# A decoder layer on one core: another engine for the first rounding, one dummy product fewer, and an even cut of the last tile

## The chip, the cores and the metric

The kernel runs on one core of a Trainium2 chip. The metric is the device time in microseconds of one execution. Three runs of the kernel before the change gave 946.8, 948.13 and 947.93 us; the median is 947.93 us.

## The reference

One layer of a decoder trunk on 512 tokens with 1024 features, in float32:

```python
h = rmsnorm(x, ln1)
q, k, v, r, a, att, gates = split(h @ w_in)
y_gla = gated_linear_attention(q, k, v, a, r) @ w_o_gla
y_att = dilated_attention(att) @ w_o_attn           # three groups of heads
x = x + (sigmoid(g_gla) * y_gla + sigmoid(g_att) * y_att) @ w_out
x = x + square(relu(rmsnorm(x, ln2) @ w_mlp1)) @ w_mlp2
x = x + sigmoid(rmsnorm(x, ln3) @ w_pg) * (p @ w_pp)
out = rmsnorm(x, ln_f)
```

Two places matter here: the very first product, 512 columns of `w_in` (the queries of the first attention group) with `x`, and the very last, `w_pg` with the normalized `x`, followed by the sigmoid gate, the addition, the last norm and the store.

## The kernel before

**Products in three terms.** TensorE multiplies operands that are rounded to fp32r. To keep float32's accuracy every operand is split into `hi`, its rounded value, and `lo`, the rounded remainder, and every product is three: hi·hi, hi·lo and lo·hi. As a rule ScalarE writes `hi` (a copy that rounds) and VectorE writes `lo` (a subtraction). Many of the middle matrix products go by a seven-product scheme on quarters of the matrices; the first and the last product do not.

**The order of the work.** The program is written out by hand in its order for each engine; every engine runs its own list in that order and waits where an operand is missing. Weights come through SyncE's DMA queue (some sums of weights through GpSimd's) a few tiles ahead of their use.

**The start (L541 to L596).** SyncE issues eight pairs of tiles, `xr[k]` (128 features by 512 tokens of transposed `x`) and `wr[k]` (128 features by 512 columns of weights), 256 KB each, and ScalarE's queue loads the small vectors `cv`. Meanwhile TensorE does `NWARM` dummy products of a 128x128 tile of ones with itself (L566). Each dummy leaves two records in the trace. Then, for each k:

- ScalarE: `xh`, the rounded `x` times the norm's weight (through `split_hi`, L476); `hi`, the rounded `wr[k]` (L579); later the square of `x` for the norm (L504).
- VectorE: the remainder of `x` (through `split_into`, L304), then `lo`, the remainder of `wr[k]` (L581); later the running sum of squares (L585).
- TensorE (L594): 12 products of 512 columns, four output tiles by three terms. For k = 0 they are sorted by term: the first four need `hi` and `xh`, the next four the remainder of `x`, the last four `lo`.

**The end (L1708 to L1772).** The last product runs tile of tokens by tile of tokens, in the order `TTS` = 2, 3, 0, 1, first for the left 512 output columns (`pg0`), then for the right ones (`pg1`). For each tile, 8 slices of features by three terms are 24 products of 512 columns. A finished tile goes through `gated_all`: `gate` on ScalarE (sigmoid, L1710), a multiplication and an addition on VectorE (L1716, L1717), the sum of squares on ScalarE (L1721). For the right half `scale_out` then finishes the norm: VectorE adds up (L1735), GpSimd takes the power (L1736), ScalarE scales the left half (L1738) and its DMA is issued, and `put` scales the right half on VectorE and stores it (L1744, L1746).

The last tile of all (L1758 to L1772) is cut at column `LAST`. Each part has its own 24 products in its own PSUM tile. The gate of the first part is issued after the first part's products, its multiplication and addition follow on VectorE, then comes the second part's gate; the squares of the first part stand on ScalarE behind that gate:

```python
    parts, sgs = [slice(0, LAST), slice(LAST, 512)], []
    for c in parts:
        ...
        sgs.append(gate(ps, n, tt))
        if c.start == 0:
            gated(sgs[0], 4 + tt, c)
    squares(sgs[0], 4 + tt, parts[0], 8)
    gated(sgs[1], 4 + tt, parts[1])
    V.tensor_scalar(sp2[:, tt:tt + 1], ss2[:, 8:9], sp2[:, tt:tt + 1], None, op0=OP.add)
    squares(sgs[1], 4 + tt, parts[1], 9)
    scale_out(tt, 9)
```

Of the kernel before, what the change touches and what calls it, by code (L numbers as in the profile page):

```python
# [13 lines left out]
AF = mybir.ActivationFunctionType  # L14
# [165 lines left out]

NRAW = 8

LAST = 384

TTS = (2, 3, 0, 1)

NWARM = 9


@with_exitstack  # L190
def block_kernel(ctx, tc, xT, x, ws, pT, wts, wha, wa2, vec, lnf, rel, onehot, ident_d, mask_d, out):
    nc = tc.nc
    V, S, TE, SY, GP = nc.vector, nc.scalar, nc.tensor, nc.sync, nc.gpsimd
# [15 lines left out]
    def u32r(name="ur"):  # L209
        return ar.tile([P, T], F32R, tag="u", name=name)  # L210
# [4 lines left out]
    def smt():  # L215
        return sm.tile([P, T], F32, tag="sm", name="smt")
# [254 lines left out]
    def split_hi(x, col=None):  # L471
        hi = u32r()
        if col is None:
            S.activation(hi, x, AF.Copy)  # L474
        else:
            S.activation(hi, x, AF.Copy, scale=col)  # L476
        return hi

    def split_lo(x, hi, col=None):
        lo = u32r()  # L480
        split_into(lo, x, hi, col)
        return hi, lo
# [18 lines left out]
    def square(x):  # L501

        t = u32()
        S.activation(t, x, AF.Square, scale=1.0 / 32.0)  # L504
        return t
# [42 lines left out]
    xr, wr = [], []  # L548
# [15 lines left out]
    pw = smt()  # L564
    for _ in range(NWARM):
        TE.matmul(pw[:, 0:P], lhsT=ones, rhs=ones, start=True, stop=True)  # L566
# [8 lines left out]
    for k in range(KC):  # L575
        x, ln = xr[k], cv[:, C_LN1 + k:C_LN1 + k + 1]
        hi, lo = u32r(), u32r()
        xh = split_hi(x, ln)
        S.activation(hi, wr[k], AF.Copy)  # L579
        xsr.append(split_lo(x, xh, ln))  # L580
        V.tensor_tensor(lo, wr[k], hi.bitcast(F32), op=OP.subtract)  # L581
        if k == 1:
            acc = sq
        elif k > 1:
            V.tensor_tensor(acc, acc, sq, op=OP.add)  # L585
        sq = square(x)
        xh, xl = xsr[k]

        terms = [(i, j) for i in range(NS) for j in range(3)]
        if not k:  # L590
            terms.sort(key=lambda t: t[1])
        for i, j in terms:
            c = slice(i * P, (i + 1) * P)
            TE.matmul(q0ps[i], lhsT=(hi, hi, lo)[j][:, c], rhs=(xh, xl, xh)[j], start=not k and not j,  # L594
                      stop=k == KC - 1 and j == 2)
# [1161 lines left out]

    parts, sgs = [slice(0, LAST), slice(LAST, 512)], []  # L1758
    for c in parts:
# [101 lines left out]
```

## Time and profile before

| | |
|---|---|
| median of three runs | 947.93 us (946.8 to 948.13) |
| the profiled execution | 946.6 us |
| its span in the profile | 944.8 us |
| TensorE, products | 936.2 us busy, 5860 records |
| VectorE | 737.9 us busy |
| ScalarE | 555.6 us busy |
| GpSimd | 113.2 us busy |
| DMA | 158.75 MB, 168 GB/s on average |

The profile is of one execution; its times are counted from the start of the span. PE is TensorE's products, PEld its loads of the stationary operand, DVE VectorE, ACT ScalarE, POOL GpSimd, SPq, ACTq and POOLq the queues in which SyncE, ScalarE and GpSimd issue DMAs. A row of the timeline gives the start, the duration, the engine, the line, the operation, the tiles written and read, their shapes, how many instructions are merged in it, and in brackets the engine's idle time before it and what ended that. A row of the grouped view gives the count, the total busy time, the mean duration in ns, and idle time. Products are pipelined, so their durations overlap; their pace is read from the distances of their starts.

### The profile page before, as it was taken

To read this page: it belongs to the slowest core of one execution; us is meant where nothing else is said; L and a number is where in the kernel's file an instruction comes from. 1 tells how busy PE (TensorE), PEld (TensorE's weight loads), DVE (VectorE), ACT (ScalarE), POOL (GpSimd) and SP (SyncE) were. 2 spreads that over 40 slices of the span, in tenths; PEclk is the share of its full clock that TensorE was granted. 3 is DMA by queue.
4 is the path that set the end of the run, shared out by engine and by line. 5 is a ranking of instruction groups with operands and counts; after the bars stand their busy time and mean duration, and the time that the engine had idled before them with its cause. 6 is when DMAs were issued, how large, how long until landed. Compare 5 with 4: busy or idle time off the path is not lost.

```text
span 944.8 us, 15151 instructions
## 1 busy us (share of the span) xinstructions
PE 936.2 (99%) x5860; PEld 844.8 (89%) x5860; DVE 737.9 (78%) x1040; ACT 555.6 (59%) x918; POOL 113.2 (12%) x157
## 2 busy tenths in 40 slices
PE   9999999999999999999999999999999999999996
PEld 8789998899988888999988889999999888888886
DVE  7698869866789579978968779776677789897664
ACT  7357546545675578775743578665556536655543
POOL 0150010120100012022100300100000101021000
PEclk9999999999999999999999999999999999999999
DMA  9474482873817456555654788666546718599202
GB/s 356 141 234 113 133 202 68 280 237 109 189 58 212 166 134 201 135 134 179 183 148 116 177 216 256 161 172 179 157 112 166 191 49 194 148 268 368 88 1 90
DMA packets 49354, 158.75 MB, mean 168 GB/s; under 512 B 7108, under 2 KB 7696, under 8 KB 49281
## 3 DMA queue, kind: packets, MB, share of 16 engines
q1 hardware_dynamic: 31104, 103.76, 31.6%
q0 software_dynamic: 14496, 49.51, 26.5%
q10 hardware_dynamic: 3680, 4.51, 1.3%
q8 instruction: 46, 0.75, 0.3%
q14 instruction: 28, 0.22, 0.1%
HBM read 149.32 MB, written 10.26 MB: 169 GB/s over the span
## 4 chain that ended last, share of the span: by engine, by line
PE 96%; issue 1%; DVE 1%; DMA 1%; ACT 0%; POOL 0%; POOLq 0%; DVEq 0%; ACTq 0%
PE mmt L338 75%; PE smt L338 12%; PE mmt L594 2%; PE smt L1028 2%; DMA u<-y_dram 1%; PE smt L968 1%; PE smt L891 1%; PE smt L566 0%; PE smt L861 0%; PE smt L985 0%; PE smt L984 0%; PE smt L860 0%; PE smt L974 0%; PE smt L1412 0%; PE smt L1084 0%
## 5 line engine op out<-in xcount | busy, mean ns | idle before, releaser
L338 PE MATMUL mmt<-ur,hi 128*128 128x256 f32 (+1 forms) x2192 | 436.4, 297 | 0.0
L338 PEld LDWEIGHTS mmt<-ur,hi 128*128 128x128 f32 x2192 | 349.7, 189 | 11.8
L302 DVE TENSOR_TENSOR lo<-w,hi 128x1024 fp32r<-128x1024 f32 x254 | 308.6, 1219 | 60.5 <-PE mmt L338 37.0
L338 PE MATMUL mmt<-ur,lo 128*128 128x256 f32 (+1 forms) x1096 | 326.6, 298 | 0.5 <-DVE lo L302 0.5
L324 ACT ACTIVATE hi<-w 128x1024 fp32r<-128x1024 f32 x254 | 265.4, 1055 | 101.9 <-PE mmt L338 24.8
L338 PE MATMUL mmt<-hi,ur 128*128 128x512 f32 (+3 forms) x912 | 266.2, 375 | 0.0
L338 PEld LDWEIGHTS mmt<-ur,lo 128*128 128x128 f32 x1096 | 206.6, 189 | 6.3 <-DVE lo L302 0.7
L338 PEld LDWEIGHTS mmt<-hi,ur 128*128 128x128 f32 x912 | 165.3, 188 | 28.6
L338 PE MATMUL mmt<-lo,ur 128*128 128x512 f32 (+3 forms) x456 | 170.6, 374 | 0.0
L474 ACT ACTIVATE ur<-u 128x512 fp32r<-128x512 f32 x113 | 67.5, 625 | 65.3 <-DVE u L622 17.1
L338 PEld LDWEIGHTS mmt<-lo,ur 128*128 128x128 f32 x456 | 85.7, 188 | 15.1
L338 PE MATMUL smt<-hi,ur 128*128 128x512 f32 x288 | 89.1, 390 | 0.0
L302 DVE TENSOR_TENSOR ur<-u,ur 128x512 fp32r<-128x512 f32 x112 | 73.6, 685 | 10.8 <-ACT ur L474 10.2
L467 DVE TENSOR_TENSOR u<-u,mmt 128x512 f32<-128x512 f32 (+1 forms) x94 | 58.0, 648 | 27.2 <-PE mmt L338 26.9
L253 POOL DMA_DIRECT2D w<-in_wts_dram x46 | 43.5, 993 | 249.8 <-DMA w<-in_wts_dram 145.3
L408 ACT ACTIVATE u<-mmt 128x512 f32<-128x512 f32 x72 | 42.9, 596 | 51.0 <-PE mmt L338 50.8
L338 PEld LDWEIGHTS smt<-hi,ur 128*128 128x128 f32 x288 | 53.8, 188 | 10.9
L338 PE MATMUL smt<-lo,ur 128*128 128x512 f32 x144 | 56.0, 389 | 0.0
L281 POOL DMA_DIRECT2D w<-in_wts_dram x18 | 16.1, 894 | 282.0 <-DVE w L278 158.1
L338 PEld LDWEIGHTS smt<-lo,ur 128*128 128x128 f32 x144 | 27.0, 188 | 5.7
L1509 ACT ACTIVATE u<-u 128x512 f32<-128x512 f32 x24 | 15.0, 628 | 26.7 <-DVE u L1505 26.7
L844 ACT ACTIVATE u<-u,st 128x256 f32<-128x256 f32 (+1 forms) x32 | 15.6, 488 | 12.5 <-DVE st L840 11.0
(242 smaller groups left out, 848.0 us busy)
## 6 DMA issues: line engine op xcount, KB each, us to landing
w<-in_wts_dram SPq DMA_DIRECT2D x182, 512.0 KB, 5.1
w<-in_wts_dram POOLq DMA_DIRECT2D x70, 512.0 KB, 7.1
u<-in_xT_dram SPq DMA_DIRECT2D x8, 256.0 KB, 5.2
u<-in_ws_dram SPq DMA_DIRECT2D x8, 256.0 KB, 5.3
v_dram<-u ACTq DMA_DIRECT2D x8, 256.0 KB, 6.4
u<-v_dram POOLq DMA_DIRECT2D x8, 256.0 KB, 6.5
y_dram<-u ACTq DMA_DIRECT2D x8, 256.0 KB, 2.2
u<-y_dram POOLq DMA_DIRECT2D x8, 256.0 KB, 7.0
```

The lines of the kernel that those rows point to most:

```text
L253: GP.dma_start(w, wts[UNIT[b]], accum_op=OP.add)
L281: GP.dma_start(w, wts[UNIT[f"{q}.A21"]], accum_op=OP.add)
L302: V.tensor_tensor(lo, x, hi.bitcast(F32), op=OP.subtract)
L324: S.activation(hi[:, s], w[:, s], AF.Copy, scale=1.0 if c is None else c)
L338: TE.matmul(o, lhsT=l, rhs=r, start=a, stop=b, skip_group_check=shared)
L408: S.activation(sums[c], bank[b], AF.Copy, scale=-scale if c[0] else scale)
L467: V.tensor_tensor(out, s, ps, op=OP.subtract if m else OP.add)
L474: S.activation(hi, x, AF.Copy)
L594: TE.matmul(q0ps[i], lhsT=(hi, hi, lo)[j][:, c], rhs=(xh, xl, xh)[j], start=not k and not j, stop=k == KC - 1 and j == 2)
L844: S.activation(q3[:, a, s:], q3[:, a, s:], AF.Exp, bias=nm[:, col + a:col + a + 1], accum_out=sums[:, col + a:col + a + 1])
L1028: TE.matmul(o, lhsT=l[a][:, lc], rhs=r[b], start=start and i == 0, stop=stop and i == 2)
L1509: S.activation(s, s, AF.Square)
```

## The change

Three edits. In the first round of the start (k = 0) VectorE writes `hi` of the weights with `tensor_copy`, in its list ahead of the remainder of `x`; rounds 1 to 7 stay with ScalarE. There are 8 dummy products instead of 9. And the last tile of tokens is cut at column 256 instead of 384, so that both parts have 256 columns.

```diff
-LAST = 384
+LAST = 256
...
-NWARM = 9
+NWARM = 8
...
         xh = split_hi(x, ln)
-        S.activation(hi, wr[k], AF.Copy)
+        if k:
+            S.activation(hi, wr[k], AF.Copy)
+        else:
+            V.tensor_copy(hi, wr[k])
         xsr.append(split_lo(x, xh, ln))
         V.tensor_tensor(lo, wr[k], hi.bitcast(F32), op=OP.subtract)
```

## The prediction, made before the changed kernel was run

> **What bounds the kernel now.** I read the page first, then the chain of work that ended last, then the timeline of the two ends that the change touches: the first 9 us and the last 15.
>
> ```profile
> span 944.8 us, 15151 instructions
> PE 936.2 (99%) x5860; PEld 844.8 (89%) x5860; DVE 737.9 (78%) x1040; ACT 555.6 (59%) x918; POOL 113.2 (12%) x157
> PEclk9999999999999999999999999999999999999999
> PE 96%; issue 1%; DVE 1%; DMA 1%; ACT 0%; POOL 0%; POOLq 0%; DVEq 0%; ACTq 0%
> ```
>
> TensorE is busy 99% of the span and is 96% of the chain. So between its first product and its last one, work on other engines is worth nothing, and a shift of the first product is carried to the end. What can move the time is what lies before the first real product and after the last one, and how long the products take. The profiled execution took 946.6 us around its span of 944.8; the median of the three runs is 947.93 (946.8 to 948.13), 1.33 us more than the profiled one. I make the sum on the profiled execution and take its difference off the median.
>
> **The start.** Order of time on the chain, then the engines' rows around the first product (the page's timeline, start and duration in us):
>
> ```profile
> 1.00 4.21 PE smt L566 x18
> 5.21 22.16 PE mmt L594 x96
> ...
> 1.19 0.42 SPq L554 DMA_DIRECT2D u<-in_ws_dram  x1
> 3.76 0.72 ACT L476 ACTIVATE ur<-u,cv 128x512 fp32r<-128x512 f32 x1 [0.89 <-DMA cv<-in_vec_dram]
> 4.39 0.61 ACT L579 ACTIVATE ur<-u 128x512 fp32r<-128x512 f32 x1
> 4.52 0.75 DVE L304 SCALAR_TENSOR_TENSOR ur<-u,cv,ur 128x512 fp32r<-128x512 f32 x1 [3.65 <-ACT ur L476]
> 5.19 0.68 DVE L581 TENSOR_TENSOR ur<-u,ur 128x512 fp32r<-128x512 f32 x1
> ...
> 4.57 0.63 PE L566 MATMUL smt<-ones 128*128 128x128 f32 x2
> 4.79 0.42 PE L566 MATMUL smt<-ones 128*128 128x128 f32 x1
> 5.06 0.74 PE L594 MATMUL mmt<-ur 128*128 128x512 f32 x1
> 5.63 0.63 PE L594 MATMUL mmt<-ur 128*128 128x512 f32 x2
> 5.86 0.63 PE L594 MATMUL mmt<-ur 128*128 128x512 f32 x2
> ...
> u<-in_ws_dram SPq DMA_DIRECT2D x1, 256.0 KB, 3.1
> L1058 DVE COPY u<-u 128x256 f32<-128x256 f32 x4 | 1.2, 288 | 0.0
> L1505 DVE TENSOR_SCALAR u<-u 128x512 f32<-128x512 f32 x32 | 13.5, 424 | 0.5
> ```
>
> Nine dummies are 18 records, one every 0.21 us (4.57 to 4.79). The last takes its slot to about 5.00. The rounded weights `hi` come from ScalarE at 4.39 + 0.61 = 5.00. So two things release the first product at 5.06 at once, and taking away either alone gains nothing: the diff moves both.
>
> *One dummy fewer*: two records, 2 x 0.21 = 0.43 us; the array is free at 4.57.
>
> *Rounding on VectorE*: the tile lands at 1.19 + 3.1 = 4.29, and VectorE idles until 4.52, so the copy starts near 4.33. Its cost with an fp32r result has no row. Nearest are a plain copy of half the size (0.288) and a one-operand instruction of the same size in f32 (0.424); the upper bound is L581, two operands and an fp32r result, 0.68. I take 0.42, since the copy also reads one operand: `hi` at 4.75, first product at about 4.80, 0.25 us earlier. With 0.68 it would be ready at 5.01: nothing gained, 0.01 lost. The other operand is ready at 3.76 + 0.72 = 4.48, the floor, and would allow 0.5 us. The Trainium skill, "VectorE: DVE Perf Modes", section "Mode 2×_2P", says that a copy with a single source in SBUF gets two results a cycle even in fp32, while two-tensor instructions stay at one; the row for 256 columns (0.288, against 0.42 for two operands below) agrees for f32, and no run here shows it for an fp32r result.
>
> Behind the copy on VectorE stand L304 and L581 of the first tile. L304 goes from 4.52 to about 4.77, L581 ends near 6.12 instead of 5.87. Their readers are the fifth and the ninth product, which at 0.23 us a product after 5.86 come at 6.3 and 7.2: hidden. ScalarE loses 0.61 us of work, and its later tiles come no later. No DMA is moved past another; SP's and POOL's queues are untouched.
>
> *How much of 0.25 us survives.* The first product took from 5.06 to 5.63, the next from 5.63 to 5.86: the array was still slow until somewhere in that gap, though the page's clock line shows 9 throughout. The weight loads say the same:
>
> ```profile
> L566 PEld LDWEIGHTS smt<-ones x18: 288/333/338, 1.0 to 4.6; 128*128 128x128 f32 x18
> L594 PEld LDWEIGHTS mmt<-ur x96: 187/188/338, 5.1 to 26.8; 128*128 128x128 f32 x96
> ```
>
> If the clock rises at the same moment as now, products started earlier run slowly. At twice 0.227 us the second would start at 5.25 and the third at 5.71 instead of 5.86: 0.15 us gained. With the 0.57 us of the present first gap it is 5.37 and 5.82, 0.04 gained; with a clock already up, 0.25. I take 0.15 (bounds -0.05 to 0.25).
>
> **The end.** The last tile of tokens: first 24 products of 384 columns, then 24 of 128, then the way out.
>
> ```profile
> 930.83 0.34 PE L338 MATMUL mmt<-lo,ur 128*128 128x384 f32 x1
> ...
> 934.50 0.33 PE L338 MATMUL mmt<-lo,ur 128*128 128x384 f32 x1
> ...
> 934.91 0.27 PE L338 MATMUL mmt<-lo,ur 128*128 128x128 f32 x1
> ...
> 937.25 0.28 PE L338 MATMUL mmt<-lo,ur 128*128 128x128 f32 x1
> 937.36 0.28 PE L338 MATMUL mmt<-hi,ur 128*128 128x128 f32 x1
> 937.68 0.37 ACT L1710 ACTIVATE u<-mmt,rt 128x128 f32<-128x128 f32 x1 [1.82 <-PE mmt L338]
> 938.08 0.29 DVE L1716 TENSOR_TENSOR u<-u 128x128 f32<-128x128 f32 x1 [1.04 <-ACT u L1710]
> 938.40 0.29 DVE L1717 TENSOR_TENSOR u<-u 128x128 f32<-128x128 f32 x1
> 938.73 0.31 ACT L1721 ACTIVATE u<-u 128x128 f32<-128x128 f32 x1 [0.18 <-DVE u L1717]
> 939.16 0.21 DVE L1735 TENSOR_SCALAR sp<-ss,sp 128x1 f32<-128x1 f32 x1 [0.35 <-ACT u L1721]
> ...
> 199.81 0.28 PE L338 MATMUL mmt<-lo,ur 128*128 128x256 f32 x1
> ...
> 202.66 0.28 PE L338 MATMUL mmt<-lo,ur 128*128 128x256 f32 x1
> ```
>
> Each `lo` row stands for three products. Eight groups of 384 columns: 930.83 to 934.50 is 7 steps, 0.524 for three, 0.175 each. Eight of 128: 934.91 to 937.25 is 7 steps, 0.334, so 0.111 each. A third of the columns still costs 64% of the time: a narrow product does not get below its floor. At 256 columns, from 199.81 to 202.66 there are 8 groups of three: 0.119 each.
>
> *Products.* From the second to the last there are 46 intervals, now 937.36 - 930.83 = 6.53 us; at 0.119 they are 5.47. That saves 1.06, plus 0.05 for the first interval: 1.1 us. The last product ends at 937.64 - 1.1 = 936.54.
>
> The Trainium skill, "TensorE: Matmul & The Clock Gate", section "Back-to-back issue gap", gives an isolated gap of N/2.4 + 2.5 ns (and itself says that it counts too little at small N). By it 24 products of 384 and 24 of 128 take 24 x (162.5 + 55.8) ns = 5.24 us, an estimate from that page, and 48 of 256 take the same 5.24: nothing would be saved here, and the change would cost what follows. The 0.111 us of the 128-column rows is against it.
>
> *The way out.* What follows the last product is now on 256 columns instead of 128, and each step waits for the one before. Rows of 256 columns:
>
> ```profile
> L1420 ACT ACTIVATE u<-smt,cv 128x256 f32<-128x256 f32 x16 | 6.3, 474 | 3.8 <-PE smt L1412 3.8
> L1176 DVE TENSOR_TENSOR u<-u 128x256 f32<-128x256 f32 x16 | 6.0, 418 | 0.0
> L1263 ACT ACTIVATE u<-u 128x256 f32<-128x256 f32 x32 | 11.4, 411 | 19.1 <-DVE u L467 19.1
> ```
>
> Gate 0.474 - 0.37 = 0.10; multiply and add 2 x (0.418 - 0.29) = 0.26; squares 0.411 - 0.31 = 0.10: 0.46 us longer. The end gains 1.1 - 0.46 = 0.64 us (0.5 to 0.75 with the roundings of these rows).
>
> *The first part.* It has the cover of the third tile's way out:
>
> ```profile
> 930.86 0.69 ACT L1710 ACTIVATE u<-mmt,rt 128x512 f32<-128x512 f32 x1 [0.90 <-PE mmt L338]
> ...
> 934.66 0.73 ACT L1738 ACTIVATE u<-u,fr 128x512 f32<-128x512 f32 x1 [0.90 <-POOL fr L1736]
> 935.29 0.56 ACT L1710 ACTIVATE u<-mmt,rt 128x384 f32<-128x384 f32 x1
> ```
>
> ScalarE takes its first gate only behind L1738, at 935.29, so finishing those products 1.3 us earlier brings nothing forward. The gate ends at 935.76, multiply and add (2 x 0.42 and two hops of 0.03) at 936.67; the second gate ends at 936.58 + 0.47 = 937.05. VectorE is free 0.4 us before it is wanted. Had it no such room, at most 0.84 us of that work would come onto the path, more than the gain; this is the place to look at. The first part's squares lie beside the second multiply and add, as now. From L1735 on (power, scaling, three output DMAs) nothing changes.
>
> **Sum.** 0.15 + 0.64 = 0.8 us off: 946.6 to 945.8 for the profiled execution, 947.93 to 947.1 for the median. That is 0.08%, below the 0.2% (1.9 us) that a measurement of this kernel can tell from no change.
>
> **The rivals.**
>
> 1. *VectorE's rounding takes 0.68 us, or something else holds the first product*: that part of the change then does not do what it says. It leaves 0.64 us: 947.3. For it: no row of an fp32r copy. Against: 0.424 for one operand of this size. 0.12.
>
> 2. *The clock rises later (slower than before).* Place: with 8 dummies the array has nothing from 4.57 to 4.80, where now the break is some 0.06 us (5.00 to 5.06). Work at half pace loses half a us for each us of delay. From the first dummy to the rise it now takes some 4.6 us (1.00 to about 5.6); were that wait repeated, 2.3 us would be lost, 1.5 net: 949.4. It is slower than before from a delay of 1.6 us on, and by over 0.2% from 5.4 us on. For it: the slow rows up to 5.06. Against: 0.23 us is 5% of the 4.6. 0.06. The Trainium skill, "TensorE: Matmul & The Clock Gate", Part 1, speaks of a free-running window of about 3.4 us that must be busy; by that one missed window would cost an estimated 1.7 us; no row here shows the window.
>
> 3. *Time goes by columns*, so that the products save nothing: 0.46 - 0.15 = 0.3 us slower, 948.2. The 128-column rows are against it. 0.02.
>
> 4. *The start gains all that the other operand allows* (0.5 us, with the clock up early): 0.5 + 0.64: 946.8. 0.06.
>
> **How the numbers follow.** Forecast 0.70, rivals 0.12, 0.06, 0.02 and 0.06; 0.04 is left for what I don't see, split over both sides. No case named reaches 1.9 us by itself; beyond that bound I leave 0.04 for faster (a low median on top of rival 4), 0.04 for slower (rival 2 with a longer delay), and 0.92 within. The bounds of the unknown costs give -0.05 + 0.5 to 0.25 + 0.75: 946.9 to 947.5; the spread of the three runs (1.1 below their median, 0.2 above) widens that to 945.8, and rival 2 pulls the other end to 948.7.
>
> **What would show it.** First L594 product near 4.80 and the second one still slow; a copy at L582 of some 0.42 us from 4.33; 16 dummy records. At the end, 48 products at 0.119 us, the last ending about 5.7 us after the third tile's gate starts (now 937.64 - 930.86 = 6.8); a gate of 0.47 us that waits for TensorE and not for VectorE. Wrong would be: a multiply of the second part that waits for the first part's add, slow weight loads after 6 us, or a copy of 0.7 us.

## The result

22 runs of each kernel, taken by turns: 946.21 us (945.21 to 947.49) with the change, 947.39 us (946.8 to 949.93) before; ratio 0.9986, 95% interval 0.9979 to 0.9992. Measured again later: 946.69 against 946.70, ratio 0.9998 (0.9990 to 1.0007). The forecast of 0.8 us, a ratio of 0.9992, lies just at the edge of the first interval and inside the second; both measured differences are below the 0.2% that the prediction names as the least that can be told from no change.

The profiled execution of the changed kernel took 946.66 us, where the profiled one of before took 946.6. So the two traces show no gain at all, and they show why: from the 101st product to the last tile the changed one took 0.66 us longer (903.75 against 903.09), which gave back the 0.59 us that the end had won. The page of the changed kernel:

```profile
span 944.9 us, 15147 instructions
PE 935.0 (99%) x5858; PEld 843.1 (89%) x5858; DVE 738.3 (78%) x1041; ACT 555.5 (59%) x917; POOL 113.5 (12%) x157
```

TensorE works 1.2 us less, and the span is as long as before. The three places, from the timeline of the changed kernel; first the start:

```profile
1.18 0.42 SPq L554 DMA_DIRECT2D u<-in_ws_dram  x1
3.87 0.72 ACT L476 ACTIVATE ur<-u,cv 128x512 fp32r<-128x512 f32 x1 [0.98 <-DMA cv<-in_vec_dram]
4.41 0.43 DVE L582 CAST ur<-u 128x512 fp32r<-128x512 f32 x1 [3.54 <-DMA u<-in_ws_dram]
4.76 0.74 DVE L304 SCALAR_TENSOR_TENSOR ur<-u,cv,ur 128x512 fp32r<-128x512 f32 x1
4.99 0.77 PE L597 MATMUL mmt<-ur 128*128 128x512 f32 x1 [0.21 <-DVE ur L582]
5.55 0.68 PE L597 MATMUL mmt<-ur 128*128 128x512 f32 x2
5.42 0.69 DVE L584 TENSOR_TENSOR ur<-u,ur 128x512 fp32r<-128x512 f32 x1
```

The copy takes 0.43 us and ends at 4.84; the first product starts at 4.99, 0.07 earlier than before, the second at 5.55 instead of 5.63, the third at 5.83 instead of 5.86. The end:

```profile
931.41 0.28 PE L338 MATMUL mmt<-lo,ur 128*128 128x256 f32 x1
...
936.93 0.28 PE L338 MATMUL mmt<-hi,ur 128*128 128x256 f32 x1
935.93 0.46 ACT L1713 ACTIVATE u<-mmt,rt 128x256 f32<-128x256 f32 x1
936.42 0.42 DVE L1719 TENSOR_TENSOR u<-u 128x256 f32<-128x256 f32 x1 [0.37 <-ACT u L1713]
936.88 0.42 DVE L1720 TENSOR_TENSOR u<-u 128x256 f32<-128x256 f32 x1
937.75 0.42 DVE L1719 TENSOR_TENSOR u<-u 128x256 f32<-128x256 f32 x1 [0.45 <-ACT u L1713]
938.21 0.42 DVE L1720 TENSOR_TENSOR u<-u 128x256 f32<-128x256 f32 x1
938.67 0.42 ACT L1724 ACTIVATE u<-u 128x256 f32<-128x256 f32 x1 [0.55 <-DVE u L1720]
939.22 0.21 DVE L1738 TENSOR_SCALAR sp<-ss,sp 128x1 f32<-128x1 f32 x1 [0.45 <-ACT u L1724]
939.51 0.54 POOL L1739 TENSOR_TENSOR fr<-sp,mh 128x1 f32<-128x1 f32 x1 [4.24 <-DVE sp L1738]
```

From the second product to the last are 936.93 - 931.41 = 5.52 us, 0.120 each; before it was 6.53. From the last product's end (937.21) to L1738 it is 2.01 us; before, from 937.64 to L1735, 1.52. VectorE idles 0.45 us before the second multiplication: the first part was out of its way, as forecast.

And the middle. In the changed kernel TensorE waits here for VectorE (first fence), in the kernel with only the last tile cut, profiled later, it does not (second fence; the names of lines differ by three):

```profile
542.53 2.01 ACT L324 ACTIVATE hi<-w 128x1024 fp32r<-128x1024 f32 x2 [7.66 <-DMA w<-in_wts_dram]
548.29 1.28 DVE L467 TENSOR_TENSOR u<-u,mmt 128x512 f32<-128x512 f32 x2
549.03 0.33 PE L1415 MATMUL smt<-ident,u 128*128 128x128 f32 x1 [0.74 <-DVE u L467]
549.63 0.98 PE L1415 MATMUL smt<-ident,u 128*128 128x128 f32 x7 [0.27 <-DVE u L467]
...
DMA to landing us min/median/max: 12.9/12.9/12.9
```

```profile
546.72 1.28 DVE L467 TENSOR_TENSOR u<-u,mmt 128x512 f32<-128x512 f32 x2
547.87 1.17 PE L1412 MATMUL smt<-ident,u 128*128 128x128 f32 x8
...
DMA to landing us min/median/max: 11.6/11.6/11.6
```

The last row of each is for one transfer of weights that GpSimd issues at L319 near 529.5 us. It lands 1.3 us later in the first; ScalarE waits for it, VectorE for ScalarE's list, and TensorE for VectorE's L467. The profiled execution of before had a smaller stall in another place, which the changed one does not have. There the chain goes back to loads of `y_dram`: their median time to landing is 7.0 us in this execution and 6.2 in the changed one.

```profile
443.10 0.39 PE L338 MATMUL mmt<-ur,lo 128*128 128x256 f32 x1 [0.48 <-DVE lo L302]
```

### The profile page after: what moved, and what is told of

Same layout as the page of the kernel before. It is cut to its first block, busy times and chain, and to the rows that moved or that the text cites. A ratio compares the mean times of both kernels' runs of the same rounds, so it can differ in the third digit from the quotient of the medians.

```text
span 944.9 us, 15147 instructions
## 1 busy us (share of the span) xinstructions
PE 935.0 (99%) x5858; PEld 843.1 (89%) x5858; DVE 738.3 (78%) x1041; ACT 555.5 (59%) x917; POOL 113.5 (12%) x157
## 3 DMA queue, kind: packets, MB, share of 16 engines
q10 hardware_dynamic: 3680, 4.51, 1.3%
## 4 chain that ended last, share of the span: by engine, by line
PE 95%; DMA 2%; DVE 1%; issue 1%; ACT 1%; POOL 0%; POOLq 0%; DVEq 0%; SPq 0%; ACTq 0%
PE mmt L338 74%; PE smt L338 11%; PE mmt L597 2%; PE smt L1031 2%; DMA w<-in_wts_dram 1%; PE smt L971 1%; PE smt L894 1%; PE smt L988 0%; PE smt L864 0%; PE smt L977 0%; PE smt L863 0%; PE smt L987 0%; PE smt L1187 0%; PE smt L1087 0%; DMA u<-in_ws_dram 0%
## 5 line engine op out<-in xcount | busy, mean ns | idle before, releaser
L338 PE MATMUL mmt<-hi,ur 128*128 128x512 f32 (+1 forms) x912 | 265.2, 374 | 0.0
L338 PE MATMUL mmt<-lo,ur 128*128 128x512 f32 (+1 forms) x456 | 170.2, 373 | 0.0
L467 DVE TENSOR_TENSOR u<-u,mmt 128x512 f32<-128x512 f32 (+1 forms) x94 | 58.0, 649 | 27.2 <-PE mmt L338 26.9
```

Source lines behind the costliest of these rows:

```text
L338: TE.matmul(o, lhsT=l, rhs=r, start=a, stop=b, skip_group_check=shared)
L467: V.tensor_tensor(out, s, ps, op=OP.subtract if m else OP.add)
```

## The experiments

Theory A: the gain is what the last tile gives (0.6 us) and a tenth or two from the start; the rest of the distance between the medians is spread. Theory B: the change itself is worth 1.2 us or more, most of it at the start. The table has what the traces of all kernels show (us). "Copy to product" is from the end of the rounding of the first weights to the first real product; "middle" from the 101st real product to the first of the last tile; "landing" is the longest of L319's transfers issued between 520 and 535 us; "last tile" is from the start of its first product (an interval ahead of the first `lo` row) to the last power on GpSimd.

| kernel | first product | copy to product | middle | landing | last tile | ratio to before |
|---|---|---|---|---|---|---|
| before | 5.06 | 0.06 | 903.09 | 11.5 | 8.80 | |
| whole change | 4.99 | 0.15 | 903.75 | 12.9 | 8.21 | 0.9986 (0.9979 to 0.9992) |
| tail_only | 5.03 | 0.06 | 902.45 | 11.6 | 8.20 | 1.0000 (0.9991 to 1.0009) |
| start_only | 4.93 | 0.14 | 903.95 | 13.1 | 8.79 | 1.0005 (0.9996 to 1.0014) |
| copy_only | 4.86 | 0.14 | 902.44 | 11.6 | 8.79 | one run: 945.79 us |
| dummy_only | 5.17 | 0.05 | 902.45 | 11.6 | 8.79 | one run: 946.13 us |
| one_wait | 4.82 | 0.06 | 903.71 | 12.8 | 8.21 | 0.9988 (0.9978 to 0.9997) |
| nwarm4 | 4.86 | 0.14 | 903.57 | 11.4 | 8.21 | 1.0004 (0.9995 to 1.0013) |
| cut128 | 4.88 | 0.14 | 904.12 | 13.3 | 9.82 | 1.0012 (1.0001 to 1.0022) |
| cut320 | 4.88 | 0.14 | 902.51 | 11.6 | 8.40 | 0.9984 (0.9975 to 0.9994) |
| after_again | 5.24 | 0.14 | 904.09 | 13.2 | 8.20 | 0.9998 (0.9990 to 1.0007) |
| one_wait_again | 5.00 | 0.05 | 903.94 | 13.0 | 8.21 | 1.0006 (0.9997 to 1.0014) |
| tail_again | 5.17 | 0.05 | 902.48 | 11.6 | 8.20 | 0.9998 (0.9990 to 1.0007) |
| copy_tail | 4.95 | 0.14 | 904.03 | 13.2 | 8.20 | 1.0001 (0.9993 to 1.0010) |

**The parts alone.** tail_only:

```diff
-LAST = 384
+LAST = 256
```

> The kernel before with only the last tile cut at 256. Theory A (the gain sits in the last tile): the products of the last tile take about 5.9 us from the start of the first of them to the end of the last, where the kernel before took 7.0, and from there to the last L1735 it takes 2.0 us instead of 1.5; the time is 0.6 us lower, a ratio near 0.9994. First real product at 5.06 as before. Theory B (most of the gain sits in the start, and the profiled execution hid it): the same rows, but this kernel alone should then be within 0.3 us of the kernel with the whole change only by chance; start_only should show the larger gain.

start_only (the whole change with `LAST = 384`):

> The kernel before with VectorE rounding the first tile of weights and 8 dummies; the last tile stays at 384 and 128. Theory A: first real product near 4.99, second near 5.55, and from the fifth product on it runs 0.07 us ahead of the kernel before; a gain of under 0.1 us, not visible in the time (ratio 0.9995 to 1.0005). Theory B: 0.5 us or more off, ratio at most 0.9995, with products that run at least 0.3 us ahead in the trace.

The last tile is 0.6 us shorter wherever it is cut at 256 (8.20 or 8.21 against 8.79 or 8.80, eight profiled kernels against four): that part of theory A is shown in the traces. In the times it is not: tail_only's ratio is 1.0000, with an interval (0.0018 wide, 1.7 us) that holds both 0.6 us less and none. start_only's first product starts at 4.93 and its second at 5.50, ahead of before; but the array was slow for longer in that execution, and the products fell behind:

```profile
5.92 0.63 PE L597 MATMUL mmt<-ur 128*128 128x512 f32 x1
6.35 0.62 PE L597 MATMUL mmt<-ur 128*128 128x512 f32 x1
6.78 0.66 PE L597 MATMUL mmt<-ur 128*128 128x512 f32 x2
```

They come every 0.43 us until 6.8 instead of every 0.23. Its 18th product starts at 9.79, against 9.30 before. So start_only did not run 0.07 us ahead as theory A said, nor 0.3 as B said; in this trace the later change of pace cost more than the edit could give.

**The halves of the start.** copy_only has 9 dummies and the copy; dummy_only has 8 and ScalarE's rounding.

> VectorE rounds the first tile of weights, 9 dummies stay, last tile at 384 and 128. Both theories: the dummies hold the array to 5.00, so the first real product starts no earlier than 5.02; with the copy ready at 4.84 the wait for two engines is over by then. Gain 0.00 to 0.04 us. If the first product starts before 5.0, the reading that the ninth dummy holds it is wrong.

> 8 dummies, ScalarE still rounds the first tile of weights, last tile at 384 and 128. The array has nothing from 4.57 to 5.06 (0.5 us). Theory A: first real product at 5.06 as before, the clock still rises near 5.6 us: the slow weight loads end by 5.65; time unchanged. Rival of the prediction (a break makes the clock rise later): weight loads of 0.33 us go on after 6 us, and each us of delay costs half a us.

```profile
4.29 0.43 DVE L582 CAST ur<-u 128x512 fp32r<-128x512 f32 x1 [3.42 <-DMA u<-in_ws_dram]
4.78 0.42 PE L566 MATMUL smt<-ones 128*128 128x128 f32 x1
4.86 0.77 PE L597 MATMUL mmt<-ur 128*128 128x512 f32 x1
```

These rows are copy_only's. Its first product starts 0.08 us after the start of the ninth dummy's last record. Both theories expected no start before 5.02, and that was wrong: the last dummy does not hold the array for another 0.21 us. What it waits for is the copy (4.72) and 0.14 us more. In dummy_only the first product waits for ScalarE as before (4.51 + 0.61 = 5.12, product at 5.17):

```profile
PE mmt L594 <- ACT ur L579: 0.4, 1, 0.4
```

0.4 us of nothing; its third product starts at 6.05 and from there they come every 0.23 us. In this trace the pace doubles at about 5.9, against 5.6 before. That is no long delay, but one trace does not settle the rival of the later clock (see below). copy_tail takes the whole change with 9 dummies:

> The whole change but with 9 dummies. If the ninth dummy costs nothing (as the first product at 4.86 in copy_only says): first real product at 4.85 to 5.0, 0.14 us after the copy ends, and the time of the whole change. If it holds the array to 5.0, as the prediction has it: first product no earlier than 5.0 and 0.1 us lost, not visible in the time.

Its first product starts at 4.95, 0.14 after the copy, as in copy_only, and the ratio is 1.0001. In these two traces the ninth dummy does not hold the first product back, so taking it away frees nothing.

**Where the 0.14 us come from.**

```diff
-        xh = split_hi(x, ln)
         if k:
+            xh = split_hi(x, ln)
+        else:
+            xh = u32r()
+            V.tensor_scalar(xh, x, ln, None, op0=OP.mult)
```

> The whole change, and VectorE also writes the first tile's xh (a one-operand multiplication by the norm's column) ahead of the copy, so that both operands of the first product come from one engine. In the kernels with the copy, the first product starts 0.14 us after the copy ends; with ScalarE's rounding 0.05. Theory W (the second engine to be waited for costs the difference): here it starts 0.05 to 0.07 us after the copy ends. Theory L (VectorE's result reaches TensorE late): 0.14 us as before. The copy ends 0.43 us after the later of the weights' landing and the multiplication (about 0.49 us from the landing of the norm's columns near 3.8). The gain against the whole change is under 0.1 us, not visible in the time.

```profile
3.77 0.49 DVE L582 TENSOR_SCALAR ur<-u,cv 128x512 fp32r<-128x512 f32 x1 [2.89 <-DMA cv<-in_vec_dram]
4.33 0.43 DVE L586 CAST ur<-u 128x512 fp32r<-128x512 f32 x1
4.82 1.43 PE L601 MATMUL mmt<-ur 128*128 128x512 f32 x5 [0.44 <-DVE ur L586]
```

0.06 us after the copy's end, against 0.14 or 0.15 in the eight kernels whose first product needs ScalarE and VectorE. Theory W holds: waiting for a second engine costs 0.08 us. The trace of the whole change has a wait instruction of its own for it in TensorE's load queue, which the kernel before has not:

```profile
L597 PEldq EVENT_SEMAPHORE  x1: 51/51/51, 4.9 to 4.9; - x1
```

As a version to use it is not shown to be better: 0.9988 on one chip, 1.0006 on another.

> The whole change with both operands of the first product from VectorE. First product 0.06 us after the copy ends, about 0.08 us ahead of the whole change; time equal to the whole change within 0.1 us by every theory, so the two ratios should differ by no more than their intervals.

**The clock.** nwarm4 is the whole change with `NWARM = 4`.

> The whole change with 4 dummies. The array has nothing from about 2.9 to 4.9 us. Theory G1 (the clock rises after some time of steady work, counted from its start): the rise comes 2 us or more later than in the kernels with 8 or 9 dummies (4.5 to 6.8 us), at 8 us or later; products of 0.43 us go on until then, and the time is 1 to 2 us higher than with the whole change. Theory G2 (the rise comes at times of its own, whatever TensorE did in the last 2 us): the rise lies in the range seen, 4.5 to 6.8 us, and the time is that of the whole change.

These rows are nwarm4's:

```profile
4.86 0.77 PE L597 MATMUL mmt<-ur 128*128 128x512 f32 x1 [1.78 <-DVE ur L582]
...
7.55 0.63 PE L597 MATMUL mmt<-ur 128*128 128x512 f32 x1
7.98 0.58 PE L597 MATMUL mmt<-ur 128*128 128x512 f32 x1
8.40 0.63 PE L597 MATMUL mmt<-ur 128*128 128x512 f32 x2
```

The products come every 0.43 us until 8.4, then every 0.23. With 8 or 9 dummies the pace doubled between 3.8 us (one_wait, where the last dummies already come every 0.11 us) and 7.0 us (one_wait_again, the same kernel). The moments are read from the pace alone; the profile's clock line is 9 throughout. The first fence is one_wait's, the second one_wait_again's; each row stands for the products under way at one moment, and the distances of the starts give the pace:

```profile
3.50 0.54 PE L566 MATMUL smt<-ones 128*128 128x128 f32 x2
3.72 0.55 PE L566 MATMUL smt<-ones 128*128 128x128 f32 x3
3.88 0.50 PE L566 MATMUL smt<-ones 128*128 128x128 f32 x3
4.10 0.28 PE L566 MATMUL smt<-ones 128*128 128x128 f32 x1
```

```profile
6.44 0.88 PE L601 MATMUL mmt<-ur 128*128 128x512 f32 x2
6.87 0.68 PE L601 MATMUL mmt<-ur 128*128 128x512 f32 x2
7.16 0.63 PE L601 MATMUL mmt<-ur 128*128 128x512 f32 x2
7.39 0.62 PE L601 MATMUL mmt<-ur 128*128 128x512 f32 x2
```

So for a break of 2 us one trace is as G1 has it, later than all thirteen others. In that execution it cost, at the 18th product, 10.47 against 9.28 in the whole change, 1.2 us. The times fit: nwarm4 took 947.56 us where one_wait, on the same chip, took 945.96. The Trainium skill, "TensorE: Matmul & The Clock Gate", Part 1, has the clock rise after a busy window of about 3.4 us that runs freely and doesn't start with the kernel. In that the traces agree: the moment differs in executions of the same code, and it came 3.5 us after the first product of nwarm4, where the time before was mostly empty. But that page of the Trainium skill has the moment vary by 0.5 us either way, and here it varied by 3.2 us; and one_wait's came 2.8 us after the first dummy, sooner than a whole window of work.

Do the short breaks with 8 dummies delay it too? Estimated from the pace, it came at 4.5 (tail_only), 5.2 (tail_again), 5.5 (copy_tail), 5.6 (copy_only) and 5.6 (before) with 9 dummies, and at 3.8 (one_wait), 3.9 (after_again), 4.0 (cut128), 5.7 (whole change), 5.9 (dummy_only), 6.0 (cut320), 6.9 (start_only) and 7.0 (one_wait_again) with 8. Three of the eight had it before the dummies ended, so that their break can't have delayed it. In the other five it came later than in every kernel with 9 dummies. With one trace to a kernel this doesn't show a delay, but it doesn't exclude one either: rival 2 stays open for a break of 0.2 to 0.5 us.

**The cut.** cut128 and cut320 are the whole change with the last tile cut there.

> The whole change, but the last tile cut at 128: 24 products of 128 columns, then 24 of 384. By the sum of the prediction: products as in the kernel before (7.0 us from the first start to the last end, 1.07 more than at 256), and the way out on 384 columns (from the last product's end to the last power on GpSimd) longer: 1.8 us before on 128 columns, 2.3 at 256, 2.7 to 2.8 here. From the first product's start to that power: before 8.8, whole change 8.2, here 9.7 us. Time 1.5 us above the whole change.

> The whole change, but the last tile cut at 320: 24 products of 320 columns, then 24 of 192. Floor theory (a product does not get below 0.11 us): 24 x 0.147 + 24 x 0.113 and 0.2 us for the last to end, 6.4 us; the way out on 192 columns 2.05; from the first product's start to the last power 8.5 us, between the kernel before (8.8) and the whole change (8.2). Columns theory (pace by columns only): 5.9 us for the products as at 256, then 2.05, 8.0 us, better than the whole change.

```profile
931.29 0.28 PE L338 MATMUL mmt<-lo,ur 128*128 128x128 f32 x1
...
937.94 0.34 PE L338 MATMUL mmt<-hi,ur 128*128 128x384 f32 x1
941.05 0.54 POOL L1739 TENSOR_TENSOR fr<-sp,mh 128x1 f32<-128x1 f32 x1 [5.85 <-DVE sp L1738]
```

```profile
934.78 0.28 PE L338 MATMUL mmt<-lo,ur 128*128 128x192 f32 x1
...
936.12 0.28 PE L338 MATMUL mmt<-lo,ur 128*128 128x192 f32 x1
936.24 0.28 PE L338 MATMUL mmt<-hi,ur 128*128 128x192 f32 x1
938.57 0.54 POOL L1739 TENSOR_TENSOR fr<-sp,mh 128x1 f32<-128x1 f32 x1 [4.44 <-DVE sp L1738]
```

cut128 (first fence): the way out from the last product's end to the power is 941.05 - 938.28 = 2.77 us, as forecast, and the last tile takes 9.82. cut320 (second): 192 columns are 12 intervals from 934.78 to 936.12, 0.112 each, the same as 128 columns (0.111): there is a floor, and the columns theory, with 8.0 us for the tile, falls; 8.40 was measured, 8.5 expected. 256 gives the shortest last tile of the four cuts tried. The times follow only roughly: cut128 is the one ratio whose interval lies wholly above 1, and it took 1.9 us more than one_wait on the same chip, for a tile that is 1.6 us longer; but cut320, whose tile is 0.2 us longer than one_wait's, took 0.2 us less (945.78) and has the lowest ratio of all.

**Once more, on one chip.**

> The whole change once more, for its time beside the other three on one chip, and for one more trace. Theory A (0.6 us from the last tile, 0.1 to 0.2 from the start, the rest of the 1.2 us between the medians is spread): ratio 0.9990 to 0.9994, first product to last power 8.2 us, first real product at 4.85 to 5.0. Theory B (1.2 us or more belong to the change): ratio 0.9987 or lower, with products that run over 0.3 us ahead somewhere between the start and the last tile in a way that only the changed kernels show. Stalls near 443 and 549 us come in some executions, whatever the kernel.

> The kernel before with only the last tile cut at 256. Theory A: ratio 0.9992 to 0.9996 (0.6 us off, less what the start gives in the whole change), first product to last power 8.2 us. Theory B: ratio 0.9998 or higher, as its first measurement (1.0) would have it.

Theory B falls for this chip: the whole change is at 0.9998 with an interval above B's 0.9987, its last tile at 8.20 us, and its products run ahead nowhere else in a way of their own. Nor are A's 0.6 to 0.8 us seen in these times; 0.9992 and 0.9994 lie in both intervals, and so does 1. What the rounds leave open is whether the chip matters: one_wait and cut320 gave 0.9988 and 0.9984 on one chip, the four kernels of this round 0.9998 to 1.0006 on another, and one_wait, run on both, has intervals that meet only at 0.9997. The 0.9986 of the result is not explained.

The column "middle" sorts the profiled executions into three groups: 902.4 to 902.5 without a stall, 903.1 and 903.6 with the one near 443 us (before, nwarm4), and 903.7 to 904.1 with the one near 549 us. The last group is, without exception, the one in which the transfer of L319 took 12.8 us or more instead of 11.4 to 11.6. So this stall costs 1.3 to 1.7 us, more than the whole change is worth. The loads of `y_dram` behind the stall near 443 us have a median time to landing of 7.0 and 7.5 us in before and nwarm4, and 5.7 to 6.4 in the twelve others. The stall near 549 us is in 7 of the 10 profiled kernels with VectorE's copy and in none of the 4 without. Were seven stalls spread over the fourteen by chance, all four would be spared in 35 cases of 1000. The times speak against a tie to the copy: tail_only and tail_again, which have no copy, were profiled at 945.07 and 945.26 us without a stall, and 18 of their 21 other runs took at least 1.2 us longer than that, which is about what a stall costs. No trace shows what those runs had, so the tie is neither shown nor excluded. one_wait and one_wait_again differ by 0.0018 in their ratios, though both were profiled with the stall; so a kernel's one profile does not tell the time of its other runs.

## Why the prediction was right or wrong

- *No change that can be measured; 0.8 us off*: right. 947.1 was forecast for the median; it came to 946.21, with the kernel before at 947.39 beside it. That the distance of 1.2 us is the change's isn't shown: in the repetition it was 0.0. So it is right in that the change is too small to be seen; that the number came near is partly luck, since of its two terms the traces bear out only the last tile's.
- *The last tile, 0.64 us*: right by its steps. Products: 1.06 us forecast, 6.53 - 5.52 = 1.01 in the trace (0.120 each, not 0.119), and with the first interval 1.07 of 1.1. The way out: 0.46 longer forecast, 2.01 - 1.52 = 0.49. Together 0.59 us, and the last tile of every trace with this cut is shorter by as much. The rule by columns alone (rival 3) was rightly put aside: 192 columns cost what 128 do.
- *The cover of the first part*: right, with 0.45 us to spare for the forecast 0.4.
- *The copy, 0.42 us*: right, 0.43 in all ten traces that have it, so the first half of rival 1 falls. Its second half, that something else holds the first product, came true in part (the next point). The Trainium skill, "VectorE: DVE Perf Modes", section "Mode 2×_2P", gives a copy two results a cycle and a two-tensor instruction one. The trace agrees for an fp32r result: 0.43 us against the 0.69 of L584, which reads two tensors of that size.
- *First product 0.05 us after the copy*: wrong in size. It is 0.14, since two engines have to be waited for. With the landing at 4.38 instead of 4.29 that makes 4.99 of the forecast 4.80, and 0.03 us gained at the third product, just below the lower of the two estimates (0.04) for the 0.15 that was taken. Nor do the other traces show a gain of the start: the 18th product comes at 8.85 to 9.79 (mean 9.35) in the five kernels with both edits of the start and no other there, and at 9.01 to 9.30 (mean 9.16) in the three with neither.
- *The ninth dummy holds the array to 5.00*: wrong. A product of 512 columns started 0.08 us after the last dummy's record did; "both release it at once" was a coincidence in one trace, and only the rounding mattered.
- *The later clock (rival 2)*: with 2 us without work the pace doubled later than in any other trace; for the break of 0.2 to 0.5 us that the change makes it stays open. The prediction's sign for it, slow weight loads after 6 us, is in start_only and one_wait_again (0.33 us each, 0.19 later) and not in the profiled whole change. What was missed is that the moment differs by 3 us from execution to execution with the same code, and about half of that is felt as far as real products are running by then: one_wait's 18th product starts at 8.80, one_wait_again's at 9.89.
- *A shift of the first product is carried to the end, and other engines' work between is worth nothing*: too strong. Up to the stalls a shift is carried: the changed kernel is 0.02 us ahead at the 18th product and still at 443 us. But TensorE's 99% hid that two places in the middle hang on transfers that arrive in time in some executions and too late in others. A stall costs 0.6 to 1.1 us near 443 us and 1.3 to 1.7 near 549, as much as the change or more.

## What to carry to other kernels

When a tile must be cut so that the last part ends early, take the products' floor from the trace first: here 128 and 192 columns cost the same (0.111 and 0.112 us), so the narrow last part cost 1.07 us more in products and gave back only 0.49 us on the way out. Before moving a step that ends at the same moment as another, ask whether the other really holds anything: the last record's duration is not the time for which it blocks. And where an edit is worth less than a microsecond, compare the same stretches of several traces; the time of a whole execution here held a change of pace that comes anywhere within 3 us, and two stalls of 0.6 to 1.7 us that come in some executions.

## What the runs showed of the hardware that was not expected

- The array's pace doubled at 3.8 us in one execution of a kernel and at 7.0 us in another of the same kernel; with four dummies and 2 us without work, at 8.4. The profile's clock line, one digit for 24 us, is 9 throughout.
- A first product that waits for two engines started 0.14 or 0.15 us after the later one ended (eight traces); waiting for one, 0.05 or 0.06 (six).
- The same transfer (512 KB, issued at the same place of the program) took 11.4 to 11.6 us in seven profiled executions and 12.8 to 13.3 in seven others, with nothing between.
